# Small products of two mixers issued in turn over halves of the array, and two SBUF pools placed ahead of two others

## The chip, the cores and the metric

One core of a Trainium2 chip runs one program. The metric is device time in microseconds of one execution. The median of three runs of the kernel before is 985.54 us (985.49 to 986.58).

## The reference

Two decoder layers over 256 tokens of width 1024, in float32. Each layer adds a mixer and then a feed-forward part:

```
for layer in range(2):
    h = rmsnorm(x, norm1[layer])
    x = x + concat(gated_deltanet(h), forgetting_attention(h), pool_mixer(h)) @ w_out[layer]
    h = rmsnorm(x, norm2[layer])
    x = x + (swiglu(h) if layer == 0 else top2_of_8_expert_swiglu(h))
```

The delta net has 6 heads of 64 and works in chunks of 64 tokens, with a state S carried from one to the next:

```
a = tril_strict(kb @ k.T * decay);  u, w = solve(a + I, [v * beta, kb * exp(G)])
qk = tril(q @ k.T * decay)
for each of 4 chunks:
    v_new = u - w @ S
    o     = q_dec @ S + qk @ v_new
    S     = S * last + k_dec.T @ v_new
```

The attention has 6 heads of 64 over blocks of 128 queries: `softmax(q k.T / 8 + c_i - c_j, causal) @ v`, with c the running sum of log forget gates. The pool mixer subtracts x from its means over 2, 4, 8 and 16 tokens.

## The kernel before

The program has four stages: the mixer of layer 0 (`mix0`), the dense feed-forward part, the mixer of layer 1 (`mix1`) and the experts. A large product goes over the array as three float32r products (`mm3`, L251). Every weight tile is loaded by SyncE into a ring of six buffers (`raw`), then split by ScalarE into `whi` (L243) and by VectorE into `wlo` (L246), with four buffers of each (pool `split`).

A mixer projects its inputs group by group: z and gates, k, v, q of the delta net, v, k, q of the attention (`ps_fv`, `ps_fk`, `ps_fq`), and the pool input (`ps_p`). Between these large products stand the small ones of the delta net, and after the attention's projections those of the attention. All of them are float32 and show as two records a product in the trace (a transpose as one):

- `gram` (L621) makes the 64x64 products k k' and q k' of the 6 heads and 4 chunks (`ps_KK`). Heads 2m and 2m+1 lie on SBUF rows 0-63 and 64-127 (h2); the two chunks of a block of 128 tokens go to columns 0-63 and 64-127 of the array (c). It is called twice: for k with PSUM banks of tag D, and for q with those of tag F.
- `delta_keys` spreads exp(G) over channels by products with the identity (`ps_eGb`, L605).
- `delta_solve` inverts with 32x32 products (`ps_j`, `ps_l`), on four or two diagonal blocks of the array in turn.
- `delta_scan` (L713) goes through the four chunks: `ps_ks` (S with kg), `ps_v` (U with V), `ps_S` (the update of S; the output's column half alternates by head), and the output `ps_o`. Chunk c of a block uses rows and columns c*64 to c*64+63, so that all products of vt and P of a chunk lie on one quarter of the array; the products of S with qd use all rows and one column half.
- `log_decays` (L785) makes rows of 1x128 (`ps_c`), first six at partition 64, then six at partition 0.
- `attention` (L798): scores `ps_s`, softmax, transposes `ps_pt`, and `ps_fo`, two products a head, in the column half of the head.

PSUM has 8 banks: in a mixer three of tag A, three of D and two of F. `ps_vT`, `ps_eGb`, `ps_sq`, the second gram, `ps_c`, `ps_pt`, `ps_fo` and the pool's `ps_pool` share the two of F.

The order on each engine is not the order of the code. A scheduler runs a model of the program when it is built and picks, by priority and by when operands are ready in that model, which instruction comes next on each engine; the engines then run their queues in that order. Parts of the delta net stand in a `high_priority` block and go first wherever the model has them ready, with the large products between them.

Of the kernel before, what the change touches and what calls it, by code (L numbers as in the profile page):

```python
# [21 lines left out]
ALU = mybir.AluOpType  # L22
# [4 lines left out]
T = 256  # L27
# [42 lines left out]
class Cols:  # L70


    def __init__(self):
        self.parts, self.at, self.n = [], {}, 0
# [120 lines left out]
class Kernel:  # L195
    def __init__(self, ctx, tc, aps, out, dbg=None):
        self.tc, self.nc, self.d, self.out = tc, tc.nc, aps, out
        self.dbg = dbg
        pool = lambda n, b, **k: ctx.enter_context(tc.tile_pool(name=n, bufs=b, **k))
        self.cp = pool("const", 1)  # L200
        self.rp = pool("ring", RING)
        self.sp = pool("split", 4)
        self.big = pool("big", 2)
        self.sm = pool("small", 2)
        self.loads = self.more = 0
        self.guard = None
        self.phase_insts = []
# [351 lines left out]
    def delta_keys(self, kq):  # L559


        nc, wk = self.nc, self.wk
        for m in range(3):
            r = self.rnorm(kq[:, m, 0], 1.0, "D")
            self.tt(kq[:, m, 0], kq[:, m, 0], r, ALU.mult)
        B = wk.tile([128, 12, 64], F32, tag="s2", name="B", bufs=1)
        self.gram(kq, 0, B, "D")

        h0, h1 = self.c("half")[:, 0:1], self.c("half")[:, 1:2]
        Bc = wk.tile([128, 1056], F32, tag="t4", name="Bc", bufs=self.n4)  # L570
        nc.gpsimd.memset(Bc, 0.0)
        U1 = wk.tile([128, 1056], F32, tag="t4", name="U1", bufs=self.n4)
        nc.gpsimd.memset(U1, 0.0)
        nc.gpsimd.memset(U1[:, 0:1024:33], 1.0)
        bc = Bc[:, :1024].rearrange("p (i m) -> p i m", m=32)
        bi = B.rearrange("p m i -> p i m")
        nc.vector.tensor_scalar(bc[:, :, 0:12], bi[:, 0:32], h0, None, op0=ALU.mult)
        nc.vector.scalar_tensor_tensor(bc[:, :, 0:12], bi[:, 32:64], h1, bc[:, :, 0:12], op0=ALU.mult, op1=ALU.add)
        N1 = wk.tile([128, 1056], F32, tag="t4", name="N1", bufs=self.n4)
        nc.vector.transpose(N1[:, :1024], Bc[:, :1024])  # L580
        blocks = lambda x: x.rearrange("p (b i) -> p b i", b=2)[:, :, :512].rearrange("p b (i j) -> p b i j", j=32)
        nv, uv = blocks(N1), blocks(U1)
        for j in range(15):
            tmp = wk.tile([128, 128], F32, tag="tmp", name="tmp", bufs=2)
            sh = [128, 2, 15 - j, j + 1]
            tv = tmp[:, :2 * (15 - j) * (j + 1)].rearrange("p (b i r) -> p b i r", b=2, r=j + 1)
            nc.gpsimd.tensor_tensor(tv, nv[:, :, j + 1:16, j:j + 1].to_broadcast(sh), uv[:, :, j:j + 1, 0:j + 1].to_broadcast(sh), op=ALU.mult)
            u = uv[:, :, j + 1:16, 0:j + 1]
            nc.gpsimd.tensor_tensor(u, u, tv, op=ALU.subtract)  # L589

        self.No = wk.tile([128, 12, 32], F32, tag="d1", name="No", bufs=6)
        nc.gpsimd.tensor_tensor(self.No, bc[:, :, 0:12].rearrange("p i m -> p m i"),
                                self.c("join")[:, None, :].to_broadcast([128, 12, 32]), op=ALU.mult)


        ex = []
        for t in range(2):
            x = wk.tile([128, 6, 64], F32, tag="d1", name=f"eGx{t}", bufs=6)
            self.copy(x, self.eG[:, t * 6:t * 6 + 6, None].to_broadcast([128, 6, 64]))
            ex.append(x)  # L600
        eGb = wk.tile([128, 3, T], F32, tag="s0", name="eGb", bufs=1)
        for hp in range(3):
            ps = self.psF("ps_eGb")
            for t in range(2):
                self.mm(ps[:, t * 128:t * 128 + 128], ex[t][:, 2 * hp:2 * hp + 2].rearrange("p a d -> p (a d)"), self.ident)  # L605
            self.copy(eGb[:, hp], ps[:, :T])
        self.eGb = eGb
        self.kg = wk.tile([128, 3, T], F32, tag="s3", name="kg", bufs=1)
        self.tt(self.kg, kq[:, :, 0], self.eGb, ALU.mult)
        self.Kd = []  # L610
        for t in range(2):
            ps = self.psD("ps_kT")
            for m in range(3):
                nc.tensor.transpose(ps[:, m * 128:m * 128 + 128], kq[:, m, 0, t * 128:t * 128 + 128], self.ident)
            kd = wk.tile([128, 6, 64], F32, tag="d1", name=f"Kd{t}", bufs=6)
            self.tt(kd, ps[:, :W].rearrange("p (h d) -> p h d", d=64),
                    self.gd[:, t * 6:t * 6 + 6, None].to_broadcast([128, 6, 64]), ALU.mult)
            self.Kd.append(kd)
        self.B, self.U1 = B, U1

    def gram(self, kq, s, dest, tag):  # L621

        for t in range(2):
            for h2 in range(2):
                ps = self.ps(tag, "ps_KK")
                r = slice(h2 * 64, h2 * 64 + 64)
                for m in range(3):
                    for c in range(2):
                        n = slice((2 * t + c) * 64, (2 * t + c) * 64 + 64)
                        self.mm(ps[c * 64:c * 64 + 64, m * 64:m * 64 + 64], kq[r, m, 0, n], kq[r, m, s, n])  # L630
                e = slice(t * 6 + h2, t * 6 + 6, 2)
                self.tt(dest[:, e], ps[:, :192].rearrange("p (m i) -> p m i", m=3), self.E[:, e], ALU.mult)

    def delta_values(self, kq, vv):
        nc, wk = self.nc, self.wk
# [77 lines left out]
    def delta_scan(self, zs, ohi, olo):  # L713
        nc, wk = self.nc, self.wk
# [5 lines left out]
            St.append(x)  # L720
        S = None
        vt = po = None
        done = []
        def output(t, po):
            sq = wk.tile([128, 6, 64], F32, tag="d1", name="osq", bufs=6)
            nc.scalar.activation(sq.rearrange("p h d -> p (h d)"), po[:, :W], AF.Square)
# [14 lines left out]
        for n in range(4):  # L741
            t, c = divmod(n, 2)
            r = slice(c * 64, c * 64 + 64)
            ns = slice(n * 64, n * 64 + 64)
            if c == 0:
                po = self.psD("ps_o")
                vt = wk.tile([128, 6, 64], F32, tag="d1", name="vt", bufs=6)

            if S is not None:
                ps = self.psD("ps_ks")  # L750
# [3 lines left out]
            ps = self.psD("ps_v")  # L754
# [3 lines left out]
            src = vt  # L758
            if n < 3:
                ps = self.psD("ps_S")  # L760
# [4 lines left out]
                for h2 in range(2):  # L765
# [4 lines left out]
                    else:  # L770
                        self.tt(new, S[k, :, k], self.el2[k, c, t, :, None].to_broadcast([64, 3, 64]), ALU.mult)
                        self.tt(new, new, got, ALU.add)
            for m in range(3):
                if S is not None:
                    self.mm(po[r, m * 128:m * 128 + 128], self.qd[:, m, ns], S[:, m], True, False)
                for h in (2 * m, 2 * m + 1):
                    self.mm(po[r, h * 64:h * 64 + 64], self.P[r, t * 6 + h], src[r, h], S is None, S is None or h % 2 == 1)
            if n < 3:
                S = S2
            done.append(po)  # L780

        output(0, done[1])
        output(1, done[3])

    def log_decays(self, fk):  # L785

        for hs in ((0, 1), (2,)):
            ps = self.psF("ps_c")
            for h2, r in ((0, 64), (1, 0)):
                for i, hp in enumerate(hs):  # L790
                    for t in range(2):
                        o = i * T + t * 128
                        j = t * 6 + 2 * hp + h2
                        self.mm(ps[r:r + 1, o:o + 128], self.ncum[:, j:j + 1], self.ident)
                n = len(hs)
                self.copy(fk[h2][r:r + 1, hs[0]:hs[0] + n].rearrange("p m t -> p (m t)"), ps[r:r + 1, :n * T])

    def attention(self, fv, fk, fq, ohi, olo):  # L798
        nc, wk = self.nc, self.wk
        for h in range(6):  # L800
            hp, r = h // 2, slice((h % 2) * 64, (h % 2) * 64 + 64)
            ps = self.psA("ps_s")
            for t in range(2):
                o = ps[:, :128] if t == 0 else ps[:, 128:384]
                e = ps[:, :128] if t == 0 else ps[:, 256:384]
# [17 lines left out]
            ps = self.psF("ps_pt")  # L823
            for i in range(3):
                nc.tensor.transpose(ps[:, i * 128:i * 128 + 128], P[:, i * 128:i * 128 + 128], self.ident)
            PT = wk.tile([128, 384], F32, tag="f1", name="PT", bufs=4)
            self.copy(PT, ps[:, :384])
            if h % 2 == 0:
                po = self.psF("ps_fo")
            hs = slice(h * 64, h * 64 + 64)  # L830
            self.mm(po[r, :T], fv[0][:, hs], PT[:, :T], True, False)
            self.mm(po[r, 128:T], fv[1][:, hs], PT[:, T:], False, True)
            if h % 2 == 1:
                self.hi_lo(ohi[:, 3 + hp], olo[:, 3 + hp], po[:, :T])

    def pooling(self, m, ps, ohi, olo):
        nc, wk = self.nc, self.wk
# [559 lines left out]
```

## Time and profile before

| | us |
|---|---|
| median of three runs | 985.54 |
| the profiled execution's own time | 986.71 |
| its span | 984.9 |
| TensorE busy with products | 933.9 (95%) |
| VectorE, ScalarE, GpSimd busy | 724.6, 620.2, 125.7 |

The two mixers lie at about 0 to 170 us and 355 to 525 us. In both TensorE is busy nearly throughout, but with small products among the large ones; in the experts' stage, from about 600 us on, the DMA engines too are busy for nine tenths of the time and more. A busy engine is no engine at its peak: a record of a small product counts as busy for its whole length, though the next one may start long before its end. For the small products the distance from start to start counts.

### The profile page before, as it was taken

The page shows a single profiled execution, that of the slowest core. Times are in us where ns is not written, and L with a number is a line of the kernel's source. Part 1 is how long each engine was busy: PE and PEld are TensorE (multiplying, and loading weights), DVE is VectorE, ACT ScalarE, POOL GpSimd, SP SyncE. Part 2 cuts the span into 40 slices and gives each one's busy share as a digit, 9 for nine tenths or more (in the row PEclk, how much of TensorE's full clock was granted, in tenths as well). Part 3 has the DMA queues.
Part 4 walks back from the last instruction along what each step waited for, and adds up shares of the span by engine and source line. Part 5 has one row for each costly group of instructions (what it writes and reads, how often), then busy time and mean ns, then how long its engine had stood idle before and what let it go on. Part 6 is the DMA issues. An engine that isn't in the chain of part 4 may idle for free.

```text
span 984.9 us, 17481 instructions
## 1 busy us (share of the span) xinstructions
PE 933.9 (95%) x6453; PEld 824.0 (84%) x6453; DVE 724.6 (74%) x1030; ACT 620.2 (63%) x978; POOL 125.7 (13%) x195
## 2 busy tenths in 40 slices
PE   6989999999999989899997899998999999999996
PEld 6988877999999979888776789987899788988874
DVE  5877556755555557866646776988899888888895
ACT  6754645644444447655635567877788688777783
POOL 2596100000000023792000000000000000000000
PEclk9998999999999999999998999999999999999999
DMA  9524113666656537332136768999999999999991
GB/s 354 153 86 140 52 43 107 214 194 184 190 180 186 182 99 236 110 126 71 45 103 222 270 236 300 367 354 343 384 337 385 371 347 338 379 324 325 329 402 61
DMA packets 62302, 224.77 MB, mean 228 GB/s; under 512 B 6944, under 2 KB 7216, under 8 KB 62208
## 3 DMA queue, kind: packets, MB, share of 16 engines
q1 hardware_dynamic: 61632, 221.62, 65.0%
q0 software_dynamic: 576, 1.96, 0.6%
q8 instruction: 52, 0.85, 0.3%
q14 instruction: 42, 0.34, 0.1%
HBM read 222.50 MB, written 1.05 MB: 227 GB/s over the span
## 4 chain that ended last, share of the span: by engine, by line
PE 75%; DVE 9%; POOL 6%; ACT 3%; DMA 3%; issue 3%; SPq 0%; DVEq 0%; ACTq 0%; POOLq 0%
PE ps_e L249 22%; PE ps_gu L249 13%; PE ps_y L249 10%; PE ps_dn L249 6%; PE ps_out L249 5%; DVE wlo L246 4%; DMA raw<-moe 3%; PE ps_fq L249 3%; PE ps_ga L249 2%; ACT whi L243 2%; PE ps_zabf L249 2%; PE ps_o L249 1%; POOL U L589 1%; POOL cacc L527 1%; PE ps_p L249 1%
## 5 line engine op out<-in xcount | busy, mean ns | idle before, releaser
L246 DVE TENSOR_TENSOR wlo<-raw,whi 128x1024 fp32r<-128x1024 f32 (+3 forms) x386 | 471.3, 1245 | 143.3 <-ACT whi L243 139.6
L243 ACT ACTIVATE whi<-raw 128x1024 fp32r<-128x1024 f32 (+3 forms) x386 | 406.0, 1072 | 185.2 <-PE ps_e L249 48.0
L249 PE MATMUL ps_e<-wlo,gThi 128*128 128x384 f32 x448 | 156.0, 348 | 6.9 <-DVE wlo L246 6.8
L249 PE MATMUL ps_e<-whi,gThi 128*128 128x384 f32 x448 | 151.3, 344 | 2.5 <-ACT whi L243 2.0
L249 PE MATMUL ps_e<-whi,gTlo 128*128 128x384 f32 x304 | 102.6, 339 | 0.2 <-ACT gTlo L243 0.2
L249 PE MATMUL ps_gu<-hThi,whi 128*128 128x256 f32 x352 | 99.8, 283 | 1.3 <-DVE hTlo L246 1.3
L249 PE MATMUL ps_gu<-hThi,wlo 128*128 128x256 f32 x352 | 99.4, 282 | 0.0
L249 PE MATMUL ps_gu<-hTlo,whi 128*128 128x256 f32 x352 | 99.4, 282 | 0.0
L249 PEld LDWEIGHTS ps_e<-wlo,gThi 128*128 128x128 f32 x448 | 84.9, 190 | 14.1 <-DVE wlo L246 10.4
L249 PEld LDWEIGHTS ps_e<-whi,gThi 128*128 128x128 f32 x448 | 84.5, 189 | 7.5 <-ACT whi L243 3.4
L249 PE MATMUL ps_y<-wlo,ehi 128*128 128x512 f32 x192 | 74.8, 407 | 0.9 <-DVE wlo L246 0.9
L249 PEld LDWEIGHTS ps_gu<-hThi,whi 128*128 128x128 f32 x352 | 67.3, 191 | 2.5 <-DVE hTlo L246 1.5
L249 PE MATMUL ps_y<-whi,ehi 128*128 128x512 f32 x192 | 66.6, 407 | 1.7 <-DVE ehi L246 1.3
L249 PEld LDWEIGHTS ps_gu<-hTlo,whi 128*128 128x128 f32 x352 | 67.3, 191 | 1.0
L249 PEld LDWEIGHTS ps_gu<-hThi,wlo 128*128 128x128 f32 x352 | 67.3, 191 | 0.0
L249 PEld LDWEIGHTS ps_e<-whi,gTlo 128*128 128x128 f32 x304 | 57.5, 189 | 1.3 <-ACT gTlo L243 0.4
L249 PE MATMUL ps_y<-whi,elo 128*128 128x512 f32 x120 | 46.9, 395 | 0.0
L249 PEld LDWEIGHTS ps_y<-wlo,ehi 128*128 128x128 f32 x192 | 35.9, 188 | 10.1 <-DVE wlo L246 1.8
L249 PEld LDWEIGHTS ps_y<-whi,ehi 128*128 128x128 f32 x192 | 35.6, 188 | 10.4 <-DVE ehi L246 1.7
L249 PE MATMUL ps_e<-raw,gThi 128*128 128x384 f32 x96 | 35.5, 493 | 0.0
L249 PE MATMUL ps_dn<-whi,fhi 128*128 128x512 f32 x88 | 35.0, 398 | 0.0
L249 PE MATMUL ps_dn<-wlo,fhi 128*128 128x512 f32 x88 | 34.8, 396 | 0.0
(404 smaller groups left out, 1814.6 us busy)
## 6 DMA issues: line engine op xcount, KB each, us to landing
raw<-moe SPq DMA_DIRECT2D x128, 576.0 KB, 5.9
raw<-moe SPq DMA_DIRECT2D x96, 512.0 KB, 5.5
raw<-ffn SPq DMA_DIRECT2D x66, 512.0 KB, 3.6
raw<-moe SPq DMA_DIRECT2D x64, 384.0 KB, 5.8
raw<-win SPq DMA_DIRECT2D x34, 512.0 KB, 3.8
raw<-wout SPq DMA_DIRECT2D x16, 512.0 KB, 3.7
raw<-win SPq DMA_DIRECT2D x8, 402.0 KB, 4.8
raw<-win SPq DMA_DIRECT2D x4, 576.0 KB, 4.4
```

The lines of the kernel that those rows point to most:

```text
L243: return self.nc.scalar.activation(out, in_, AF.Copy, scale=scale)
L246: return self.nc.vector.tensor_tensor(out, a, b, op=op)
L249: self.nc.tensor.matmul(out, l, r, start=start, stop=stop)
L527: eng.tensor_scalar(acc, x, w[:, o + 3:o + 4], None, op0=ALU.mult)
L589: nc.gpsimd.tensor_tensor(u, u, tv, op=ALU.subtract)
```

## The change

`gram` opens both heads' tiles of a block and issues the four quarters of the array in turn. `delta_scan` gathers the output products of both chunks of a block behind the second chunk and issues them in turn. `log_decays` alternates between the two output rows. `attention` issues the `ps_fo` products of a pair of heads together, behind the second head's transposes. `ps_eGb` is made by a transpose in place of a product with the identity. And the pools `big` and `small` are opened before `ring` and `split`, which moves their addresses. The placing of the pools leaves every engine's order as it is: with the pools alone moved, the orders are those of before, and with all else changed and the pools left, those of the change.

```diff
         self.cp = pool("const", 1)
+        self.big = pool("big", 2)
+        self.sm = pool("small", 2)
         self.rp = pool("ring", RING)
         self.sp = pool("split", 4)
-        self.big = pool("big", 2)
-        self.sm = pool("small", 2)
...
-                self.mm(ps[:, t * 128:t * 128 + 128], ex[t][:, 2 * hp:2 * hp + 2].rearrange("p a d -> p (a d)"), self.ident)
+                nc.tensor.transpose(ps[:, t * 128:t * 128 + 128], ex[t][:, 2 * hp:2 * hp + 2].rearrange("p a d -> p (a d)"), self.ident)
...
         for t in range(2):
+            ps = [self.ps(tag, "ps_KK") for _ in range(2)]
+            for m in range(3):
+                for c in range(2):
+                    n = slice((2 * t + c) * 64, (2 * t + c) * 64 + 64)
+                    for h2 in range(2):
+                        r = slice(h2 * 64, h2 * 64 + 64)
+                        self.mm(ps[h2][c * 64:c * 64 + 64, m * 64:m * 64 + 64], kq[r, m, 0, n], kq[r, m, s, n])
             for h2 in range(2):
-                ps = self.ps(tag, "ps_KK")
-                r = slice(h2 * 64, h2 * 64 + 64)
-                for m in range(3):
-                    for c in range(2):
-                        n = slice((2 * t + c) * 64, (2 * t + c) * 64 + 64)
-                        self.mm(ps[c * 64:c * 64 + 64, m * 64:m * 64 + 64], kq[r, m, 0, n], kq[r, m, s, n])
...
+            states.append(S)
+            if c == 1:
+                both = [(c, slice(c * 64, c * 64 + 64), states[2 * t + c]) for c in range(2)]
+                for m in range(3):
+                    for c, r, S0 in both:
+                        if S0 is not None:
+                            ns = slice((2 * t + c) * 64, (2 * t + c) * 64 + 64)
+                            self.mm(po[r, m * 128:m * 128 + 128], self.qd[:, m, ns], S0[:, m], True, False)
+                    for h in (2 * m, 2 * m + 1):
+                        for c, r, S0 in both:
+                            self.mm(po[r, h * 64:h * 64 + 64], self.P[r, t * 6 + h], vt[r, h], S0 is None, S0 is None or h % 2 == 1)
...
-            for h2, r in ((0, 64), (1, 0)):
-                for i, hp in enumerate(hs):
-                    for t in range(2):
+            for i, hp in enumerate(hs):
+                for t in range(2):
+                    for h2, r in ((0, 64), (1, 0)):
...
+            if h % 2 == 1:
                 po = self.psF("ps_fo")
+                for r, hs, PT in pair:
+                    self.mm(po[r, :T], fv[0][:, hs], PT[:, :T], True, False)
+                for r, hs, PT in pair:
+                    self.mm(po[r, 128:T], fv[1][:, hs], PT[:, T:], False, True)
```

On TensorE, the second gram of layer 0 stands before as follows (`ps_KK_896`, `_904` and `_912` are its banks in order, `ps_sq` sums of squares, `ps_fq0` the large products, twenty in a row, of which the first and the last are shown):

```order
L249 MATMUL ps_KK_896<-kq_296 64x64 x2
L249 MATMUL ps_sq_879<-cst_70,sq_888 128x2 x2
L249 MATMUL ps_fq0_1528<-hThi_95,whi_1524 128x256
...
L249 MATMUL ps_fq0_1528<-hTlo_96,whi_1524 128x256
L249 MATMUL ps_KK_904<-kq_296 64x64 x6
L249 MATMUL ps_KK_912<-kq_296 64x64 x6
```

In the change the same place of the same engine reads (`_897` is the second head's bank of the first block, `_913` of the second; `ps_c` comes from `log_decays`):

```order
L249 MATMUL ps_KK_896<-kq_296 64x64 x2
L249 MATMUL ps_sq_879<-cst_70,sq_888 128x2 x2
L249 MATMUL ps_KK_897<-kq_296 64x64 x6
L249 MATMUL ps_KK_912<-kq_296 64x64 x6
L249 MATMUL ps_fq0_1528<-hThi_95,whi_1524 128x256
...
L249 MATMUL ps_KK_913<-kq_296 64x64 x6
L249 MATMUL ps_c_1309<-cst_70,gs_282 1x128 x8
```

The bursts of six of one head have stayed bursts of one head, and twenty large products that stood between `ps_sq` and the burst of twelve now stand behind it.

On TensorE, the output of the second block of layer 0 stands before in two places (chunk 2 with state S1, and further on chunk 3 with S0, each on its own half), the first of which begins:

```order
L249 MATMUL ps_S_1220<-vt_1206,Kd1_581 64x64 x6
L249 MATMUL ps_o_1205<-S1_1145,qd_878 64x128
L249 MATMUL ps_o_1205<-vt_1206,P_895 64x64 x2
L249 MATMUL ps_o_1205<-S1_1145,qd_878 64x128
L249 MATMUL ps_o_1205<-vt_1206,P_895 64x64 x2
```

In the change both chunks stand together, behind the last `ps_v`:

```order
L249 MATMUL ps_v_1236<-V1_876,U_1085 64x64 x6
L249 MATMUL ps_o_1205<-S1_1145,qd_878 64x128
L249 MATMUL ps_o_1205<-S0_1143,qd_878 64x128
L249 MATMUL ps_o_1205<-vt_1206,P_895 64x64
...
L249 MATMUL ps_o_1205<-S1_1145,qd_878 64x128
L249 MATMUL ps_o_1205<-S0_1143,qd_878 64x128
L249 MATMUL ps_o_1205<-vt_1206,P_895 64x64 x4
```

Where two products on one half followed one on the same half, four on two quarters now follow two on two halves.

## Rows read from the trace of the kernel before

**Rows 1.** Windows: us, busy PE, PEld, DVE, ACT, POOL, granted clock, DMA share, GB/s
```profile
84.30:94.80 10.50, 10.38 (x82) 9.31 (x82) 8.18 (x13) 5.38 (x11) 5.75 (x12) 0.67 0.31 99
94.80:110.30 15.50, 15.05 (x451) 13.19 (x451) 8.71 (x15) 6.97 (x16) 3.20 (x3) 1.00 0.23 71
110.30:155.40 45.10, 45.10 (x348) 35.03 (x346) 27.72 (x80) 25.62 (x67) 0.27 (x3) 1.00 0.14 38
439.30:449.80 10.50, 10.38 (x179) 9.37 (x180) 8.62 (x14) 5.26 (x11) 5.80 (x13) 0.84 0.31 98
```

**Rows 2.** Chain of waits, 84 to 156 us: start, us, what
```profile
94.90 1.47 PE ps_j L249 x96
...
104.19 1.40 PE ps_c L249 x12
...
112.17 0.84 PE ps_v L249 x12
...
113.63 0.51 PE ps_S L249 x12
114.15 0.69 PE ps_o L249 x12
...
116.66 0.22 PE ps_o L249 x2
...
119.95 0.79 PE ps_fo L249 x4
...
122.54 1.70 PE ps_o L249 x16
...
137.73 2.20 PE ps_o L249 x18
...
153.60 1.84 PE ps_o L249 x16
```

**Rows 3.** Timeline of TensorE, chunk 2's output: start, us, instruction, records
```profile
137.66 0.43 PE L249 MATMUL ps_o<-S,qd 128*64 128x128 f32 x2
138.03 0.44 PE L249 MATMUL ps_o<-vt,P 64*64 64x64 f32 x4
138.40 0.43 PE L249 MATMUL ps_o<-S,qd 128*64 128x128 f32 x2
```

**Rows 4.** Timeline of TensorE, second gram: idle before and its releaser last
```profile
84.31 0.33 PE L249 MATMUL ps_KK<-kq 64*64 64x64 f32 x4 [1.63 <-POOL kq L545]
84.76 0.92 PE L249 MATMUL ps_sq<-cst,sq 128*128 128x2 f32 x4
...
85.90 0.41 PE L249 MATMUL ps_fq<-hTlo,whi 128*128 128x256 f32 x1
86.11 0.41 PE L249 MATMUL ps_fq<-hThi,wlo 128*128 128x256 f32 x1
...
92.21 0.28 PE L249 MATMUL ps_fq<-hTlo,whi 128*128 128x256 f32 x1
92.32 0.28 PE L249 MATMUL ps_fq<-hThi,wlo 128*128 128x256 f32 x1
```

**Rows 5.** Timeline of VectorE, same place
```profile
85.69 0.34 DVE L246 TENSOR_TENSOR P<-ps_KK,E 128x192 f32<-128x192 f32 x1
...
87.04 0.17 DVE L654 TENSOR_SCALAR qn<-ps_sq 128x12 f32<-128x12 f32 x1
```

**Rows 6.** Groups by line and shape, TensorE: busy, mean ns, idle before and releasers
```profile
L249 PE MATMUL ps_KK<-kq 64*64 64x64 f32 x192 | 9.1, 244 | 5.0 <-POOL kq L545 3.2 <-DVE B L246 1.0 <-DVE kq L246 0.9
...
L249 PE MATMUL ps_eGb<-cst,eGx 128*128 128x128 f32 x24 | 3.5, 283 | 2.7 <-ACT eGb L243 2.7
```

**Rows 7.** Timeline of the last output of layer 0's scan, VectorE and TensorE
```profile
162.84 0.56 DVE L246 TENSOR_TENSOR og<-og,ors 128x384 f32<-128x384 f32 x1
...
163.69 0.49 PE L737 MATMUL ps_oT<-cst,og 128*128 128x128 f32 x3
```

**Rows 8.** Instructions of one tile: whi on ScalarE, ns min/median/max
```profile
L243 ACT ACTIVATE whi<-raw x386: 830/1063/1188, 10.0 to 968.8; 128x1024 fp32r<-128x1024 f32 x107, 128x1152 fp32r<-128x1152 f32 x66, 128x768 fp32r<-128x768 f32 x16, 128x804 fp32r<-128x804 f32 x4
```

More of the change, by code (lines that the diff above doesn't have):

```diff
@@ L623, in gram @@
         for t in range(2):
-            for h2 in range(2):
-                ps = self.ps(tag, "ps_KK")
-                r = slice(h2 * 64, h2 * 64 + 64)
-                for m in range(3):
-                    for c in range(2):
-                        n = slice((2 * t + c) * 64, (2 * t + c) * 64 + 64)
-                        self.mm(ps[c * 64:c * 64 + 64, m * 64:m * 64 + 64], kq[r, m, 0, n], kq[r, m, s, n])
+            ps = [self.ps(tag, "ps_KK") for _ in range(2)]
[5 more added lines that the diff above has]
+                        self.mm(ps[h2][c * 64:c * 64 + 64, m * 64:m * 64 + 64], kq[r, m, 0, n], kq[r, m, s, n])
+            for h2 in range(2):
                 e = slice(t * 6 + h2, t * 6 + 6, 2)
-                self.tt(dest[:, e], ps[:, :192].rearrange("p (m i) -> p m i", m=3), self.E[:, e], ALU.mult)
+                self.tt(dest[:, e], ps[h2][:, :192].rearrange("p (m i) -> p m i", m=3), self.E[:, e], ALU.mult)
     def delta_values(self, kq, vv):
@@ L722, in delta_scan @@
         vt = po = None
-        done = []
+        done, states = [], []
         def output(t, po):
@@ L772, in delta_scan @@
                         self.tt(new, new, got, ALU.add)
[L773 to L777, printed above, removed]
+            states.append(S)
[9 more added lines that the diff above has]
+                            self.mm(po[r, h * 64:h * 64 + 64], self.P[r, t * 6 + h], vt[r, h], S0 is None, S0 is None or h % 2 == 1)
+                done.append(po)
             if n < 3:
                 S = S2
-            done.append(po)
-        output(0, done[1])
-        output(1, done[3])
+        output(0, done[0])
+        output(1, done[1])
     def log_decays(self, fk):
@@ L794, in log_decays @@
                         self.mm(ps[r:r + 1, o:o + 128], self.ncum[:, j:j + 1], self.ident)
-                n = len(hs)
+            n = len(hs)
+            for h2, r in ((0, 64), (1, 0)):
                 self.copy(fk[h2][r:r + 1, hs[0]:hs[0] + n].rearrange("p m t -> p (m t)"), ps[r:r + 1, :n * T])
@@ L799, in attention @@
         nc, wk = self.nc, self.wk
+        pair = []
         for h in range(6):
@@ L827, in attention @@
             self.copy(PT, ps[:, :384])
-            if h % 2 == 0:
+            pair.append((r, slice(h * 64, h * 64 + 64), PT))
+            if h % 2 == 1:
                 po = self.psF("ps_fo")
[L830 to L833, printed above, removed]
+                for r, hs, PT in pair:
+                    self.mm(po[r, :T], fv[0][:, hs], PT[:, :T], True, False)
+                for r, hs, PT in pair:
+                    self.mm(po[r, 128:T], fv[1][:, hs], PT[:, T:], False, True)
                 self.hi_lo(ohi[:, 3 + hp], olo[:, 3 + hp], po[:, :T])
+                pair = []
     def pooling(self, m, ps, ohi, olo):
```

## The prediction

> **What bounds the kernel now.** I read the windows first, to see where TensorE has no slack. From 110.3 to 155.4 us, the scan and attention of layer 0, it is busy for 45.10 of 45.10 us, and from 84.3 to 110.3 for 25.43 of 26.0 [rows 1]; VectorE is busy for 27.72 and ScalarE for 25.62 of those 45.10. So in these stretches the time is what TensorE's queue takes, and a microsecond less in it is a microsecond less in the kernel, so long as its operands still arrive. Before 84.3 us it is otherwise: TensorE waits 1.63 us for GpSimd's last `kq` [rows 4], and the row of all `ps_KK` shows 3.2 us of such waits in the two layers, 1.0 and 0.9 more for VectorE [rows 6]. Layer 1 runs the same program 355 us later, so each term below counts twice unless its order differs.
>
> The chain of waits then gives the small products, with the step to the next piece in each length [rows 2]. Outputs `ps_o` of layer 0: 0.69 + 0.22 + 1.70 + 2.20 + 0.22 + 1.84 = 6.87 us (the 0.22 occurs twice). `ps_fo`: 0.79 a head, six heads. `ps_c`: twice 1.40 us for 12 records, 0.117 a record. Two rows give the worth of turns: `ps_v`, all on one quarter, takes 0.84 us for 12 records, 0.070 each; `ps_S`, same shape, with the column half alternating by head, takes 0.51, 0.043 each. Going round is thus worth up to two fifths of a record here.
>
> **The change, part by part** (times saved are negative; a layer unless said).
>
> *Outputs of the scan.* A group of one m is now one or two S products and then four products of P in turn, in the first block without a state for chunk 0. Two records of S take 0.36 us up to the next product, four of P on one quarter 0.37 [rows 3]; four times 0.070 is 0.28, so 0.09 goes to the change of shape. Eight records of P in turn: 8 x 0.043 + 0.09 = 0.43. Four records of S on two column halves lie between 0.36, side by side, and 0.36 + 2 x 0.117 = 0.59, one after the other; I take 0.45. First block 3 x (0.36 + 0.43) = 2.37, second 3 x (0.45 + 0.43) = 2.64, together 5.01 against 6.87: **-1.86**. With no overlap at all P takes 0.65 and S 0.59, sum 6.75, -0.12; with full overlap 0.34 and 0.36, sum 4.2, -2.67.
>
> *Attention.* A head's 0.79 is two records of 256 columns (0.234 each by the 0.117), two of 128, and 0.09. In turn, a product of two records on one column half can have the other half's next product beside only its second record. Four together: 0.94 + 0.09 = 1.03 in place of 1.58. But the order lets only one of six pairs run so (the first of layer 1); of the others the first product goes alone (0.56) and three follow (0.79): 1.35. So -0.55 - 5 x 0.23 = **-1.7** for both layers; bounds 0 and half of all, -4.7.
>
> *Log decays.* 24 records at 0.117 become 16 and 8 on two columns in turn, 8 x 0.117 + 0.117 and 4 x 0.117 + 0.117, 1.64 against 2.80: **-1.16**; bounds 0 and -1.40.
>
> *Grams.* The second does not do what its code says. It needs three F banks at once (`ps_sq` and two heads) and there are two, so the order keeps each head's six products together, as before: nothing gained. What does move is the burst of twelve, now right behind `ps_sq` and in front of twenty large products. Its first half needs the bank of `ps_sq`, which `qn` on VectorE frees. In the new order of VectorE `qn` stands right behind the `P` that ended at 86.03 [rows 5], so it ends at about 86.2; `ps_sq` ends at 85.68 [rows 4]. TensorE, in order, stands for about **+0.6**, with the large products queued behind it; before, they covered this. Bounds 0 and 1.5, the latter if `qn` ends where it did, at 87.21. The first gram lies where VectorE's B is waited for [rows 6] and GpSimd's chain comes later anyway: 0, within 0.3 either way.
>
> *Transposes for eGb.* Half the records of 3.5 us go, in a place where TensorE then idles 2.7 us for ScalarE's copies [rows 6]: 0; at most -1.7 for both layers, if no cover were there.
>
> *New interleaving.* The order after the change comes from a model, and softmax, scan and splits meet differently; before, no wait shows in 45.10 us. I put **+0.5** for waits that the model misses; bounds 0 and 4, four steps of the scan with about 1 us each uncovered.
>
> *Tail.* The last `og` ends at 163.40 and its transposes start at 163.69 [rows 7], so the path through VectorE there is about as long as the `ps_out` products that cover it. Those are 30 in layer 0 (before 36) and 38 in layer 1. The path's own splits wait on these products, so both shorten together: 0.
>
> *Pools.* `whi` rotates through six ring and four split addresses and shows 830 to 1188 ns over all its shapes, median 1063 [rows 8]: no sign that an address matters. 0; the bound I leave is 2 us either way over the kernel, half a percent of the 386 splits' 1.06 us.
>
> Sum for both layers: 2 x (-1.86) - 1.7 + 2 x (-1.16) + 2 x 0.6 + 2 x 0.5 = -5.5 us. The profiled execution took 986.71 us (span 984.9 and 1.8 around it), so 981.2 on its scale; it was 1.2 us above the median of 985.54, against which I forecast **980.0**.
>
> **Two rules that speak against it.** `ps_j` runs over four row groups with all outputs in one bank, and its 96 records take 1.47 us [rows 2], 0.015 each; half a `ps_v` record, as it has half the columns, is 0.035. So row groups do run beside each other into one bank. The Trainium skill, "TensorEngine Tiling (Array Packing)", Restrictions and Gotchas, states that different row tiles cannot access the same PSUM bank at the same time. By that rule the P products of both chunks, in one bank, would gain nothing (rival 1's time); the trace disagrees.
>
> `ps_S` alternates between column halves on the same rows and still takes 0.043 against 0.070 [rows 2]. The Trainium skill, "TensorE: Matmul & The Clock Gate", Part 3, states that weight loads overlap running products only when the row group differs. By it turns over columns alone (S with qd, `ps_fo`, `ps_c`) would gain nothing (rival 2's time); this row disagrees too.
>
> **The rivals.**
> 1. Rows do not overlap in one bank: P takes 0.65, the outputs 3 x 1.01 + 3 x 1.10 = 6.33, -0.54 a layer. Sum -1.1 - 1.7 - 2.3 + 2.2 = -2.9: 982.6. For it, no row of 64x64 products on both row halves exists; against it, `ps_j`.
> 2. Columns alone do not overlap: S stays at 0.59, outputs 2.37 + 3 x 1.02 = 5.43, -1.44 a layer; attention and decays 0. Sum -2.9 + 2.2 = -0.7: 984.8. Against it, `ps_S`.
> 3. The time saved turns into waits: the chain from S to `ps_ks` to `ps_v` through VectorE and ScalarE sets the pace once the output products no longer stand between its steps. The four bursts of `ps_o` that stood between moved away; the large products that take their place are as many as there are, and TensorE's sum does not change who is last. If it eats all, 985.5. For it, VectorE and ScalarE serve softmax and splits in the same queue; against it, the full 45.10 us and 3 to 4 us of other products that I count between the steps in the new order.
> 4. Slower, through the clock. After the idle of 1.63 us the large products start 0.21 us apart, those at 92.2 us 0.11 to 0.12 [rows 4]: TensorE ran at 1.2 GHz from about 85.5 to 91.9, granted 0.67 on the mean, and in layer 1 0.84 on 10.5 us [rows 1]. That costs now about 3.2 and 1.7 us. The new stand at the burst falls into this stretch. If it keeps the clock low up to 100 us and to the same place of layer 1 (455), the loss is half of 14.5 and of 15.7 us, 15.1 in place of 4.9: -5.5 + 10.2 = +4.7, 990.2. It decides from 5.5 us of added loss on. For it, the wait in front stays as it is; against it, the stand is short and 32x32 products follow soon.
>
> **How the numbers follow.** Forecast 0.62, rivals in order 0.07, 0.05, 0.11, 0.15. The bounds reach from full overlap everywhere with no waits (2 x 2.67 + 4.7 + 2.8 = 12.8 us less) to rival 4; below 974 and above 987 I leave under 2 in 10: 974 to 987. The forecast's own range is 976 to 984. No change means within 0.2%, 2 us, which is about what a measurement here can tell. Faster: most of the forecast's 0.62 and most of rival 1, 0.64; slower 0.17, rival 4 and a few waits; the same 0.19.
>
> **What would show it.** Right: in the chain of the changed kernel both blocks' outputs add up to about 5 us a layer; `ps_c` takes about 1.6; `ps_fo` below 0.79 a head; TensorE stands about half a microsecond before the burst of `ps_KK`, released by `qn`; 110 to 155 us becomes 3 to 4 us shorter with TensorE still full; dense and experts only shift. Wrong: idle rows in the scan released by VectorE or ScalarE (rival 3), a granted clock below 0.67 at 85 to 95 us or low beyond it (rival 4), unchanged steps of the records in turn (rivals 1, 2), or a splitting that takes another time (pools).

## The result, and the profile after

The changed kernel takes 974.3 us (median; 973.0 to 975.5) against 984.9 (980.5 to 986.6) for the one before: a ratio of 0.9898, 95% interval 0.9877 to 0.9919, so 8 to 12 us less. The forecast was 980.0, 5.5 less than the 985.54 it started from, with a range of its own of 976 to 984. The direction was right, but the forecast had only half of the gain. The profiled execution took 973.88 us, span 972.1.

The stages, from first and last products of each in the traces (mixer 0 ends with the first `ps_gu`, dense with the last, mixer 1 with the first `ps_ro`, the router's products, and the experts' part starts with the first `ps_e`; us):

| | mixer 0 | dense | mixer 1 | to first `ps_e` | experts and end |
|---|---|---|---|---|---|
| before | 173.5 | 182.8 | 171.4 | 11.8 | 445.5 |
| after | 169.3 | 179.0 | 170.8 | 10.7 | 442.3 |

Mixer 0 gives 4.2 us, mixer 1 only 0.6. The dense stage gives 3.8, although its instructions stand in the same order as before; that is the first thing to explain. These are single executions, and the one of before (986.71) lay 1.8 above its median. The 3.2 us of the experts' part can't be put down to the change: in the single traces of all kernels below, that part lies anywhere between 441.9 and 447.7 us, with the old pools and with the new, with the turns and without.

The windows of the changed kernel: the stretch from the second gram to `ps_j` of layer 0, on to the first `ps_s`, on to the last `ps_o`; dense; the same stretch ahead of `ps_j` in layer 1; the rest of that mixer. Columns as in [rows 1].

```profile
84.30:94.70 10.40, 9.20 (x92) 7.99 (x92) 8.24 (x13) 4.87 (x12) 6.07 (x13) 0.84 0.31 98
94.70:106.90 12.20, 12.20 (x393) 11.37 (x393) 7.41 (x13) 6.08 (x14) 3.63 (x3) 1.00 0.22 59
106.90:152.60 45.70, 45.54 (x401) 34.21 (x400) 29.57 (x83) 27.72 (x71) 0.67 (x4) 1.00 0.17 50
169.30:348.30 179.00, 178.98 (x1298) 169.39 (x1299) 104.63 (x135) 84.14 (x113) 0.00 (x0) 1.00 0.64 192
430.00:442.80 12.80, 10.43 (x92) 9.16 (x92) 9.43 (x17) 4.83 (x11) 7.33 (x16) 0.73 0.27 82
442.80:519.10 76.30, 70.88 (x860) 56.24 (x859) 47.06 (x119) 39.53 (x95) 5.13 (x8) 1.00 0.33 107
```

And of before, for the dense stage and the two stretches of layer 1:

```profile
173.50:356.20 182.70, 182.70 (x1297) 171.69 (x1298) 104.56 (x135) 84.24 (x113) 0.00 (x0) 1.00 0.62 188
439.30:448.30 9.00, 8.88 (x86) 7.96 (x87) 7.12 (x12) 5.26 (x11) 5.65 (x12) 0.81 0.35 112
448.30:527.60 79.30, 75.16 (x869) 60.01 (x868) 49.88 (x123) 39.12 (x94) 4.47 (x8) 1.00 0.31 102
```

In both kernels the dense stage has TensorE full at the full clock, with the same records and the same busy time on VectorE and ScalarE. So each product of it takes less time. From `ps_j` on, layer 1 gives 3.1 us (79.4 to 76.3), near layer 0's 4.0 (78.7 to 74.6). Ahead of `ps_j` it loses: from the last `ps_gu` to the first `ps_j` of layer 1 it takes 94.5 us where it took 92.0, and TensorE idles for 10.6 us of them where it idled for 7.7. That takes most of layer 1's gain back. (The two rows of that place don't compare like with like: the window of the changed kernel takes in TensorE's wait ahead of the second gram, and that of before starts behind its own.)

The small products, in the chain of waits of the changed kernel (start, us, what; some records are missing from the trace, as one of the second `ps_fo`), against [rows 2]:

```profile
86.43 0.74 PE ps_KK L249 x22
...
92.22 0.97 PE ps_c L249 x16
...
94.78 1.47 PE ps_j L249 x96
96.25 0.54 PE ps_c L249 x8
...
118.31 0.84 PE ps_v L249 x12
...
122.93 0.49 PE ps_S L249 x12
123.42 2.22 PE ps_o L249 x30
...
126.12 0.58 PE ps_fo L249 x2
...
129.66 0.79 PE ps_fo L249 x5
...
146.18 0.62 PE ps_o L249 x6
...
150.73 1.87 PE ps_o L249 x30
```

The outputs take 2.22 + 0.62 + 1.87 = 4.71 us where they took 6.87, and the same in layer 1 (2.22, 0.62, 1.87). `ps_c` takes 0.97 + 0.54 = 1.51 instead of 2.80, a pair of `ps_fo` 0.58 + 0.79 = 1.37 instead of 1.58. `ps_v` and `ps_j`, which the change leaves alone, take what they took. The timeline of TensorE shows the turns, against [rows 3], in the first block and in the second:

```profile
123.35 0.43 PE L249 MATMUL ps_o<-S,qd 128*64 128x128 f32 x2
123.72 0.45 PE L249 MATMUL ps_o<-vt,P 64*64 64x64 f32 x8
124.09 0.43 PE L249 MATMUL ps_o<-S,qd 128*64 128x128 f32 x2
...
151.03 0.44 PE L249 MATMUL ps_o<-S,qd 128*64 128x128 f32 x4
151.40 0.45 PE L249 MATMUL ps_o<-vt,P 64*64 64x64 f32 x8
```

Eight records of P over two row halves and two column halves take the 0.37 us (123.72 to 124.09) that four on one quarter took. Four records of S on two column halves take 0.37 us (151.03 to 151.40) where two took 0.36.

Now the dense stage. One tile's products on TensorE: ns of one, shortest, median and longest; first and last start; before, then after.

```profile
L249 PE MATMUL ps_gu<-hTlo,whi x352: 274/283/283, 173.7 to 356.1; 128*128 128x256 f32 x176
...
L249 PE MATMUL ps_dn<-wlo,fhi x88: 393/398/398, 188.9 to 361.1; 128*128 128x512 f32 x88
...
L249 PE MATMUL ps_q<-hTlo,whi x48: 280/283/364, 44.6 to 412.1; 128*128 128x256 f32 x48
...
L249 PE MATMUL ps_out<-wlo,ohi x64: 387/389/398, 135.9 to 522.9; 128*128 128x512 f32 x64
```

```profile
L249 PE MATMUL ps_gu<-hTlo,whi x352: 276/281/282, 169.5 to 348.2; 128*128 128x256 f32 x176
...
L249 PE MATMUL ps_dn<-wlo,fhi x88: 389/389/397, 184.2 to 353.1; 128*128 128x512 f32 x88
...
L249 PE MATMUL ps_q<-hTlo,whi x48: 276/276/369, 43.9 to 403.9; 128*128 128x256 f32 x48
...
L249 PE MATMUL ps_out<-wlo,ohi x64: 388/392/508, 133.2 to 514.3; 128*128 128x512 f32 x64
```

A `ps_gu` product goes from 283 to 281 ns, a `ps_dn` from 398 to 389, a `ps_q` of the mixers from 283 to 276; only `ps_out` takes longer, 392 where it took 389. The step from one start to the next says the same: over the whole stage its mean is 119.9 ns for `ps_gu` before and 117.8 after. In layer 0 the means go from 119.9 to 117.9 ns for `ps_k`, 119.9 to 115.2 for `ps_v`, 119.8 to 113.8 for `ps_q`, 119.4 to 116.7 for `ps_fk`; over some 70 products of each and fewer of `ps_fq` that is about 1.0 us a layer. How much of it reaches the time is another matter, since TensorE waits in the mixers.

### The profile page after: what moved, and what is told of

Same layout as the page of the kernel before. It is cut to its first block, busy times and chain, and to the rows that moved or that the text cites. A ratio compares the mean times of both kernels' runs of the same rounds, so it can differ in the third digit from the quotient of the medians.

```text
span 972.1 us, 17456 instructions
## 1 busy us (share of the span) xinstructions
PE 915.0 (94%) x6441; PEld 807.2 (83%) x6441; DVE 723.6 (74%) x1030; ACT 617.6 (64%) x978; POOL 128.6 (13%) x195
## 4 chain that ended last, share of the span: by engine, by line
PE 71%; DVE 10%; POOL 6%; DMA 5%; ACT 4%; issue 3%; SPq 0%; ACTq 0%; DVEq 0%; POOLq 0%
PE ps_e L249 21%; PE ps_gu L249 13%; PE ps_y L249 10%; PE ps_dn L249 6%; PE ps_out L249 5%; DMA raw<-moe 4%; DVE wlo L246 4%; ACT whi L243 2%; PE ps_zabf L249 2%; PE ps_ga L249 2%; PE ps_fq L249 2%; POOL cacc L527 2%; PE ps_p L249 1%; DVE cacc L531 1%; POOL tmp L587 1%
## 5 line engine op out<-in xcount | busy, mean ns | idle before, releaser
L249 PEld LDWEIGHTS ps_e<-wlo,gThi 128*128 128x128 f32 x448 | 84.6, 189 | 13.6 <-DVE wlo L246 10.2
L249 PEld LDWEIGHTS ps_y<-whi,ehi 128*128 128x128 f32 x192 | 36.4, 192 | 10.7 <-DVE ehi L246 2.1
```

The source lines that it names most:

```text
L249: self.nc.tensor.matmul(out, l, r, start=start, stop=stop)
```

## The experiments

Before stood at 984.2, 983.9 and 984.5 us beside the three timed groups of runs, and at 983.6 beside the single ones.

**The two halves of the change.** `e1_pools` is the kernel before with the new order of pools alone, `e2_nopools` the changed kernel with the old one:

```diff
         self.cp = pool("const", 1)
+        self.big = pool("big", 2)
+        self.sm = pool("small", 2)
         self.rp = pool("ring", RING)
         self.sp = pool("split", 4)
-        self.big = pool("big", 2)
-        self.sm = pool("small", 2)
```

> The kernel before with nothing changed but the order of the pools: big and small ahead of ring and split. Theory A (the place of the activations and weights in SBUF sets the pace of the large products: the dense stage was 3.8 us shorter after the change although no instruction of it moved, 746 of 1026 steps of ps_gu at .12 and 277 at .11 against 966 at .12 and 51 at .11): about 5 to 6 us shorter than before, 979 to 980, and a dense stage (first to last ps_gu) of about 179 us, against 182.7. Theory B (the pace of that stage differs between executions of one kernel, the pools do nothing, and the turns of the mixers brought the whole 10.6 us): the same as before, 984.9 within 2 us, and a dense stage that is 182.7 or that varies.

> The changed kernel with the pools in their old order (ring and split ahead of big and small) and all else of the change kept. Theory A: the turns alone give about what was forecast for them, 4 to 5.5 us, so 979.5 to 981, with a dense stage of 182.7 us. Theory B: 974.3 within 1.5 us, like the whole change.

`e1_pools`: 977.6 us, ratio 0.9934 (0.9914 to 0.9954), 4.5 to 8.5 us less. `e2_nopools`: 979.5, ratio 0.9944 (0.9923 to 0.9966), 3.3 to 7.6 less. The dense stage follows the pools and nothing else, 179.1 and 182.8 us; first `e1_pools`, then `e2_nopools`:

```profile
L249 PE MATMUL ps_gu<-hTlo,whi x352: 276/281/282, 172.6 to 351.3; 128*128 128x256 f32 x176
...
L249 PE MATMUL ps_dn<-wlo,fhi x88: 387/389/398, 187.3 to 356.2; 128*128 128x512 f32 x88
```

```profile
L249 PE MATMUL ps_gu<-hTlo,whi x352: 274/283/283, 169.5 to 351.9; 128*128 128x256 f32 x176
...
L249 PE MATMUL ps_dn<-wlo,fhi x88: 393/398/398, 184.7 to 356.9; 128*128 128x512 f32 x88
```

Theory B, that the pace differs between executions, falls. The pools are worth about as much as the turns, and the turns together gave what was forecast for their sum: 5.5 us by the ratio (4.6 by the medians).

**The turns one by one.** `e3_scan` does the scan's outputs alone on the kernel before, `e4_attn` the log decays and the attention's values, `e14_gram` the grams; `e13_oldgram` takes the grams out of the whole change. The cores of the edits:

```diff
+            if c == 1:
...
+                    for h in (2 * m, 2 * m + 1):
+                        for c, r, S0 in both:
+                            self.mm(po[r, h * 64:h * 64 + 64], self.P[r, t * 6 + h], vt[r, h], S0 is None, S0 is None or h % 2 == 1)
```

```diff
+            for i, hp in enumerate(hs):
+                for t in range(2):
+                    for h2, r in ((0, 64), (1, 0)):
...
+                for r, hs, PT in pair:
+                    self.mm(po[r, :T], fv[0][:, hs], PT[:, :T], True, False)
```

```diff
+            ps = [self.ps(tag, "ps_KK") for _ in range(2)]
+            for m in range(3):
+                for c in range(2):
...
+                    for h2 in range(2):
```

> The kernel before with the scan's outputs alone as in the changed kernel (both chunks of a block in one burst, rows and columns in turn). Forecast of this part 3.7 us over both layers (6.87 to 5.01 a layer); after the whole change the outputs took 4.71 in layer 0. Theory A and theory B alike: 4.3 us at most, 980.5 to 981.5; if the time comes back as waits in the scan's chain, 984 to 985.

> The kernel before with the log decays in turn over columns and the values of two heads in turn (ps_c and ps_fo), nothing else. By the forecast's terms 2.3 + 1.7 = 4.0 us over both layers: 981. With ps_c at 1.51 and a pair of ps_fo at 1.37 as read after the change the same 4.0. If turns over columns alone gave nothing, 985.

> The changed kernel with the gram products as before (one half of the rows after the other, each half its own tile), all else of the change kept. By the forecast the turns of the second gram cost 0.6 us a layer, since TensorE then waits for qn ahead of its whole burst: 1.2 us faster than the changed kernel, 973. Rival: that wait is hidden by the chain of the solve behind it, and the time is 974.3 as with the change.

> The kernel before with the gram products alone in turn. By the forecast 1.2 us slower, 985 to 985.5 against 983.9. Rival: no change.

`e3_scan`: 979.3 us, ratio 0.9948 (0.9929 to 0.9968), 3.1 to 7.0 less. `e4_attn`: 978.5, ratio 0.9942 (0.9921 to 0.9963), 3.6 to 7.8 less. From the first `ps_j` to the first `ps_gu` of layer 0, 78.7 us before, the one takes 76.1 and the other 77.6; to the first `ps_ro` of layer 1, 79.4 before, 76.6 and 78.3. By these traces the outputs give 5.3 us over both layers and the other two 2.1. `e4_attn` gained more than that in its median; the rest isn't in its mixers' scan, and its experts' part, with the same instructions, was 3.6 us shorter than that of before. So the single gains add up to more than `e2_nopools` has; both intervals are wide, and I leave that difference open.

`e14_gram`: 984.3, ratio 0.9998 (0.9989 to 1.0006): nothing. `e13_oldgram`: 976.0, ratio 0.9920 (0.9904 to 0.9936), which overlaps the whole change: no cost of the grams in turn shows either. Their rows say why the forecast of a loss failed. The gram alone (first fence) has its burst at 88.95 us, behind large products, with no wait; without the grams' turns (second fence), TensorE waits in layer 1 just as it does with them (third, the changed kernel). The wait for GpSimd's `kq` ahead of the gram is in the kernel before too (fourth):

```profile
88.95 1.19 PE L249 MATMUL ps_KK<-kq 64*64 64x64 f32 x24
```

```profile
431.96 1.19 PE L249 MATMUL ps_KK<-kq 64*64 64x64 f32 x24 [0.72 <-DVE P L246]
```

```profile
431.53 0.33 PE L249 MATMUL ps_KK<-kq 64*64 64x64 f32 x4 [1.72 <-POOL kq L545]
...
433.31 1.19 PE L249 MATMUL ps_KK<-kq 64*64 64x64 f32 x24 [0.72 <-DVE P L246]
```

```profile
439.19 0.33 PE L249 MATMUL ps_KK<-kq 64*64 64x64 f32 x4 [1.57 <-POOL kq L545]
```

The wait for `P` comes from the new interleaving that the other turns bring, not from the gram's code: in the traces it stands in every kernel with the turns of the scan (in `e3_scan` in layer 1 alone, 0.53 us) and in none without.

**What of the pools' order it is.** By the allocator's addresses every tile of ring (4608 bytes a partition), split (4608) and big (8192) is a multiple of 128 bytes; the pool `small` is 3648, that is 28 times 128 and 64 over. So what lies behind `small` stands 64 bytes off, modulo 128, from what lies ahead of it. Before, splits and activations both lie ahead; after the change `small` lies between them. `fhi` and `flo`, in the stage's own pool, lie behind it in either. The order of instructions is that of before in all of the following but the last. The bytes are a tile that nothing uses; the rest only swaps lines:

```diff
         self.big = pool("big", 2)
+        pool("pad", 1).tile([128, 16], F32, name="pad")
         self.sm = pool("small", 2)
```

```
 e5_ring_first:   ring, big, small, split
 e6_small_last:   big, ring, split, small
 e7_pad32:        32 bytes, ring, split, big, small
 e8_pad64:        64 bytes, ring, split, big, small
 e9_f:            ring, split, big, 64 bytes, small
 e10_h:           ring, split, 64 bytes, big, 64 bytes, small
 e11_split_ring:  big, small, split, ring
 e12_hf:          ring, split, 64 bytes, big, small
 e15_after_pad64: (changed kernel) big, small, 64 bytes, ring, split
```

> The kernel before with the pools in the order ring, big, small, split: the ring of raw weights stays where it was (36384 on), the two splits lie where the changed kernel has them (whi 100448, wlo 118880 on), the activations hThi and hTlo lie between them (64032 on) instead of behind. The dense stage takes 182.7 us with the pools before and 179.0 to 179.1 with those of the change. Theory A1 (the splits' place, or their offset modulo 128 bytes, which goes from 32 to 96, sets the pace): about 179. Theory A2 (the activations have to be low, at 36384, or the raw ring high): 182.7. Time 978 or 984.

> The kernel before with the pools in the order big, ring, split, small: activations where the changed kernel has them (36384 on), splits 3648 bytes lower than there (whi 96800, wlo 115232), and with that at 32 modulo 128 bytes as before the change, not at 96. Theory A1 in its form of offsets modulo 128: a dense stage of 182.7 us, 984. Theory A2, or A1 in its form of regions: 179, 978.

> The kernel before with 32 bytes more ahead of the ring: every ring, split and activation moves up by 32 bytes, and lies at 0 modulo 64 instead of 32; the order of the pools stays. If it is offsets that set the pace: a dense stage other than 182.7 us, shorter than 179 perhaps. If it is regions (which tiles lie low or high, or which share a part of the memory): 182.7 and 984 as before.

> The kernel before with 64 bytes more ahead of the ring: the splits go from 32 to 96 modulo 128 bytes, as in the changed kernel, and the activations do too, which in the changed kernel stay at 32; all keep their regions. Offsets of the splits alone: a dense stage of 179 us. The difference between the offsets of splits and activations: 182.7, as before. Regions: 182.7.

> The kernel before with 64 bytes more between big and small: splits (64032 on) and activations hThi, hTlo (100896 on) stay where they are, both at 32 modulo 128 bytes; the stage's own tiles, fhi and flo among them, move by 64 bytes and go from 96 to 32. So far the dense stage was 179 us wherever the splits lay at 96 with the activations at 32 and fhi at 96 (the changed kernel, e1_pools, e5_ring_first), and 182.7 in before, e6_small_last, e7_pad32 and e8_pad64. Theory B1 (the offset of the splits against the activations, 64 modulo 128, is what helps the products that read both): ps_gu at .12 and ps_dn at .233 as before, 182.7 us. Theory B2 (the offset of the splits against fhi, 0 modulo 128, is what helps): ps_dn at .227, ps_gu at .12 or .1177. Theory B3 (regions: the splits above some 100 KB): 182.7.

> The kernel before with 64 bytes more between split and big and 64 more between big and small: the splits stay at 32 modulo 128 bytes, the activations go to 96, fhi and flo stay at 96. Theory B1: ps_gu at .1177, a dense stage nearer to 179 than to 182.7 us. Theory B2 and B3: 182.7.

> The kernel before with the pools in the order big, small, split, ring: activations where the changed kernel has them (36384 on), splits at 72800 on, 27648 bytes lower than there and lower than in e6_small_last, but at 96 modulo 128 bytes as in the changed kernel; the ring behind them. Theories B1 and B2 (offsets): 179 us in the dense stage, about 978 in all. Theory B3 (splits above 100 KB): 182.7, 984.

> The kernel before with 64 bytes more between split and big alone: splits at 32 modulo 128 bytes, activations at 96, fhi at 32; so the splits stand to both as in the changed kernel (64 to the activations, 0 to fhi), with the order of the pools and every region as before. Theories B1 and B2: 179 us in the dense stage, about 978 in all. Theory B3: 182.7, 984.

> The changed kernel with 64 bytes more between small and ring: the order of the pools stays that of the change, but the splits go back to the offset of the activations (both 32 modulo 128 bytes). If the offset is all that the pools' order brought: a dense stage of 182.5 us instead of 179.0 and about 3.6 us more in all, 978. If the pools' order has a worth of its own: 179 and 974.3.

| | splits against activations | fhi against splits | dense us | time us |
|---|---|---|---|---|
| before | 0 | 64 | 182.8 | 984 |
| `e6_small_last` | 0 | 64 | 182.8 | 984.5, 1.0002 (0.9988 to 1.0015) |
| `e7_pad32` | 0 | 64 | 182.8 | 983.9, 0.9995 (0.9978 to 1.0012) |
| `e8_pad64` | 0 | 64 | 182.8 | 984.7, 1.0003 (0.9989 to 1.0017) |
| `e9_f` | 0 | 0 | 182.5 | 979.6, one run |
| `e15_after_pad64` | 0 | 0 | 182.3 | 979.5, 0.9959 (0.9944 to 0.9975) |
| after | 64 | 0 | 179.0 | 974.3, 0.9898 (0.9877 to 0.9919) |
| `e1_pools` | 64 | 0 | 179.1 | 977.6, 0.9934 (0.9914 to 0.9954) |
| `e5_ring_first` | 64 | 0 | 179.1 | 980.1, 0.9954 (0.9936 to 0.9972) |
| `e11_split_ring` | 64 | 0 | 178.9 | 980.5, one run |
| `e10_h` | 64 | 64 | 180.0 | 980.6, one run |
| `e12_hf` | 64 | 0 | 180.6 | 983.7, one run |

(Offsets in bytes modulo 128; single runs say little of the time, since executions of one kernel lie up to 6.7 us apart, but the length of the dense stage repeats within 0.3 us for one pair of offsets, `e12_hf` excepted.)

Regions are out: `e11_split_ring` has its splits 27648 bytes lower than the change and is as short, `e6_small_last` has them 3648 bytes lower and is as long as before. The absolute offset is out too (`e7_pad32`, `e8_pad64`), and the ring's place (`e5_ring_first`). What is left is the offset of the splits against the activations. `ps_gu`, which reads both, follows it each time. `e6_small_last`, `e11_split_ring`, `e9_f`, `e10_h`, `e12_hf`, in this order:

```profile
L249 PE MATMUL ps_gu<-hTlo,whi x352: 274/283/283, 173.5 to 356.0; 128*128 128x256 f32 x176
...
L249 PE MATMUL ps_dn<-wlo,fhi x88: 388/395/398, 188.8 to 360.9; 128*128 128x512 f32 x88
```

```profile
L249 PE MATMUL ps_gu<-hTlo,whi x352: 276/281/283, 171.7 to 350.3; 128*128 128x256 f32 x176
...
L249 PE MATMUL ps_dn<-wlo,fhi x88: 389/389/397, 186.3 to 355.2; 128*128 128x512 f32 x88
```

```profile
L250 PE MATMUL ps_gu<-hTlo,whi x352: 278/283/283, 170.0 to 352.2; 128*128 128x256 f32 x176
...
L250 PE MATMUL ps_dn<-wlo,fhi x88: 392/392/404, 185.2 to 357.1; 128*128 128x512 f32 x88
```

```profile
L251 PE MATMUL ps_gu<-hTlo,whi x352: 276/279/283, 172.6 to 352.3; 128*128 128x256 f32 x176
...
L251 PE MATMUL ps_dn<-wlo,fhi x88: 388/394/398, 187.6 to 357.2; 128*128 128x512 f32 x88
```

```profile
L250 PE MATMUL ps_gu<-hTlo,whi x352: 276/279/285, 171.9 to 352.2; 128*128 128x256 f32 x176
L250 PE MATMUL ps_dn<-wlo,fhi x88: 387/392/402, 186.7 to 357.1; 128*128 128x512 f32 x88
```

This product of `ps_gu` has a median of 283 or 284 where the offset is 0 and 279 to 281 where it is 64. The mean step over the stage's `ps_gu`, of which its time is made, is 119.9 to 120.2 ns at 0 and 117.8 to 118.2 at 64. `ps_dn` doesn't follow one offset: its row has 389 in the layouts of the change, 392 to 398 in all others, whichever of its two operands the padding moved. So theory B1 (the offset of the splits against the activations) holds for `ps_gu`, B2 (the offset of the splits against `fhi`) fails for `ps_dn`, and what sets that one is open.

`e12_hf` shows that this matters: both offsets are those of the changed kernel and `ps_gu` has its pace (117.9 ns), yet the dense stage takes 180.6 us, as `ps_dn` stays slow, and its one run took the time of before. So the two columns of the table don't say all. Counted modulo 256 bytes, its activations and its `fhi` both lie 128 bytes further from the splits than in the changed kernel; whether that is the reason, no run tested.

`e15_after_pad64` closes it for the changed kernel: its order of pools, its turns, and 64 bytes that put the splits back in line. It takes 979.5 us, what `e2_nopools` takes, and its products in the dense stage show it:

```profile
L250 PE MATMUL ps_gu<-hTlo,whi x352: 278/284/287, 169.2 to 351.1; 128*128 128x256 f32 x176
...
L250 PE MATMUL ps_dn<-wlo,fhi x88: 389/393/397, 184.3 to 356.0; 128*128 128x512 f32 x88
```

So the order of the pools as such shows no worth of its own; the 64 bytes are worth 5.2 us between these two medians. The dense stage has 3.3 of them. In its mixers, though, `ps_k` keeps the median of 281 ns that it has in the changed kernel, against 283 before; so the rule of the offset is shown for `ps_gu` alone. The traces don't place the rest of the 5.2 us. The mixers are no longer with the 64 bytes (169.0 and 170.2 us, against 169.3 and 170.8 in the changed kernel; with the old pools, in `e2_nopools`, mixer 0 takes 169.3 too), and the 3.1 us between the two experts' parts (445.5 and 442.3) are no more than it differs by between traces of one layout (445.5 in before, 441.9 in `e4_attn`).

## Why the prediction was wrong, step by step

**Pools: the step that failed.** "No sign that an address matters. 0; the bound I leave is 2 us either way." The runs put 4.5 to 8.5 us there (`e1_pools`), all of it faster; 3.7 of it is the dense stage, which comes out the same in every kernel with the splits and activations placed as in the change (178.9 to 179.1 us, but for `e12_hf`); the rest the traces don't place. I looked at [rows 8], the splits on ScalarE, which indeed don't change (1063 ns in the middle before, 1062 after). The effect sits in the engine that reads the splits: TensorE, at its limit for the whole dense stage, so that 2 ns of a product count over 1056 of them and 5 to 9 ns over 264 more. The trace of before held only a faint sign of it: in `ps_k` of layer 0, 69 of 71 steps between products of one shape are 120 ns, and in `ps_fk` 13 of some 65 are 116 to 118. I asked what a moved pool does to who waits, and not what it does to the time of a product.

**Outputs of the scan: right.** Forecast 5.01 us a layer, measured 4.71. P in turn takes 0.37 for eight records (forecast 0.43): products on two row halves and two column halves overlap fully, in one bank. That is where the Trainium skill, "TensorEngine Tiling (Array Packing)", Restrictions and Gotchas, has different row tiles unable to access one PSUM bank at the same time; for these products the trace disagrees, by half their time. S takes 0.37 for four records on two column halves (forecast 0.45).

**Log decays and attention: right as steps.** 1.51 against 1.64 and 1.37 against 1.35; the fall of `ps_c` from 0.117 to 0.061 a record (0.97 over 16) and the four records of S show that turns over columns alone overlap. So rivals 1 and 2 fall, and with rival 2 the consequence that the prediction drew from the rule on weight loads. In the time, `ps_c` shows (15.5 to 14.3 us from `ps_j` to the first `ps_s` of layer 0 in `e4_attn`), `ps_fo` doesn't (63.2 and 63.3 on from there).

**Second gram: the size near, its cause wrong.** TensorE stands for 0.73 us ahead of the burst where 0.6 was forecast:

```profile
86.43 0.74 PE L249 MATMUL ps_KK<-kq 64*64 64x64 f32 x24 [0.73 <-DVE P L246]
```

```profile
86.04 0.34 DVE L246 TENSOR_TENSOR P<-ps_KK,E 128x192 f32<-128x192 f32 x1
86.30 0.15 DVE L656 TENSOR_SCALAR qn<-ps_sq 128x12 f32<-128x12 f32 x1
```

The profile names `P` (ends 86.38) as the releaser, not `qn`. And the step blamed the gram's turns, while `e13_oldgram` has the wait without them and `e14_gram` has them without the wait: it belongs to the interleaving.

**New interleaving: right in sign, in another place.** Hardly in the scan (in layer 0 TensorE is busy for 45.54 of 45.70 us; in layer 1 its idle time from `ps_j` to the first `ps_ro` grows from 4.1 to 5.4 us while the stretch gets shorter, so rival 3 falls as well) but ahead of `ps_j` in layer 1: from the last `ps_gu` to the first `ps_j` 92.0 us before, 94.5 after. The five kernels with the turns of the scan have 93.5 to 94.7 there, the twelve without 91.7 to 93.4. TensorE's waits in that stretch add up to 7.4 us before and 10.4 after. What grew most is the wait for VectorE's `kq` ahead of the first gram (0.4 to 1.4) and the new one for `P` (0.7); the wait for GpSimd's `kq` ahead of the second gram is nearly as long before (1.57) as after (1.72). The sum of waits doesn't set the length alone, though: `e2_nopools` has 94.5 us with 8.9 of waits, `e10_h` 91.7 with 10.2. So which wait costs the 2.5 us stays open.

**Transposes for eGb, tail, clock.** No run has the transposes alone, and nothing in any run speaks for a worth of them. Rival 4 did not come: the granted clock at the second gram of layer 0 rose from 0.67 [rows 1] to 0.84; over the whole stretch ahead of `ps_j` in layer 1 it is 0.94 before and 0.93 after.

So the sum of -5.5 for the turns stands against -5.5 measured (-7.6 to -3.3, `e2_nopools`), and the missing half of the gain is the pools' term. That the sum fits so well is partly luck. The forecast counted every term in both layers alike, some 2.8 us each; in the trace of `e2_nopools` mixer 0 is 4.2 us shorter than before and mixer 1 is 0.6 longer, as the outputs of the scan gave more than forecast and the interleaving took more back.

## What to carry to other kernels

When a change moves tiles in SBUF, compare the median of the large products one tile at a time before and after, not only who waits for whom: where TensorE is full, a few ns a product can be the largest term. If a trace shows one shape at two paces and the same clock, try an offset of 64 bytes between the tiles that are read together; it costs 64 bytes. Do not count on it blindly: with padding alone on the kernel before, `e10_h` and `e12_hf` shortened the dense stage by 2.7 and 2.2 us, and of their single runs one was 3.0 us faster and one no faster. And small products that fill a quarter of the array should go round rows and columns, even into one bank.

## What the hardware showed that was not expected

- The offset between stationary and moving tile in SBUF, 0 or 64 modulo 128 bytes, changes the length of a product of 256 columns: 283 or 284 ns against 279 to 281 (`ps_gu`), and in the changed kernel 276 against 283 before (`ps_q`). With the change in `ps_dn`, whose rule was not found, the dense stage moves by 3.8 us, 2%.
- What collides was not found. In the trace of before, steps of `ps_gu` take 120.0 ns on the mean while VectorE and ScalarE both work (591 steps) and 117.2 while neither does (26 steps); after, 117.1 and 117.5 (596 and 6). That hints at the other engines' accesses as the other party, but no run took them away, so it is not shown.
- Row halves and column halves overlap in one PSUM bank: eight records of 64x64 in 0.37 us, 0.046 each, against 0.093 each for four on one quarter in the same place [rows 3].
